# RMSNorm with Swish on one core: three engines from straight code to loops of three units, and the row sums shared out anew

## The chip, the core and the metric

The kernel runs on one core of a Trainium2 chip. The core has a matrix engine (TensorE), a vector engine (VectorE, DVE in the profile), an activation engine (ScalarE, ACT), a general engine (GpSimd, POOL) and SyncE (SP), which here only issues transfers. Each engine runs its own instruction stream; they meet through semaphores. Sixteen DMA engines move data between the chip's memory (HBM), where the inputs and the output lie, and the core's SBUF, 128 partitions wide. A small second memory, PSUM, also has 128 partitions.

The metric is the device time of one execution in microseconds, lower is better. One execution was also profiled; the profile's span runs from the first instruction to the last.

## The reference

```python
x = randn(16, 1024, 512)  # float32; gamma: ones(512); eps = 1e-5
rms = np.sqrt(np.mean(x ** 2, axis=-1, keepdims=True) + eps)
x_norm = x / rms * gamma
return x_norm * (1.0 / (1.0 + np.exp(-x_norm)))
```

There are 16,384 rows of 512 numbers, 2 KB each. Every row is divided by the root of its mean square, multiplied by gamma and passed through Swish, y·sigmoid(y), which the activation engine has as one function, Silu. 33.5 MB come in and 33.5 MB go out, and every row needs one sum and two passes over its data.

## The kernel before

Each partition works on 128 rows of its own, numbered 0 to 127 in the order in which they are worked on. The rows lie in HBM in four groups (`groups = [32, 48, 20, 28]`): in a group of n rows each partition has n neighbouring rows, so that a transfer of some of them is one contiguous piece per partition. SBUF holds a ring of 100 rows per partition (`xb`); row r lies at place r modulo 100. Everything is done in place: x is loaded into the ring, normalized there, passed through Silu there, and stored from there.

Four rows of every partition make a unit; there are 32 (`K`). A unit k goes through five steps:

- `square(k)` on ScalarE waits for the loads that the unit needs (L200). Two rows are squared one by one into PSUM with an accumulator that leaves their mean squares in `ms` (L203; the accumulator is read by an instruction of its own). The other two are squared together into a PSUM tile `sq` (L210).
- `sums(k)` on VectorE reduces that PSUM tile to the other two mean squares (L241).
- GpSimd adds eps (L184) and raises to the power -0.5 (L191), which gives `rstd` for four rows.
- `norm(k)` on VectorE multiplies each of the four rows by its rstd and by gamma (scalar_tensor_tensor, L252).
- `swish(k)` on ScalarE runs Silu over the four rows at once (L222).

All loops are Python loops, so that each engine has one long straight program. ScalarE's order is square(0), square(1), square(2), swish(0), square(3), swish(1) and so on; VectorE's is sums(0), sums(1), norm(0), sums(2), norm(1) and so on. Most waits are part of the waiting instruction and count upwards: `s_norm` at least k + 1, for instance. `ms`, `aeps` and `rstd` have a place for each unit; the PSUM tiles are two of each kind.

Three alignment directives stand at the head of the program (L151): the code of ScalarE, VectorE and GpSimd is placed at slots 8, 40 and 0 of a block of 128 instructions, and the engines jump there.

SyncE issues all data transfers in the written `order`. The first two loads go out ahead of the start-up barrier. Then come the loads up to row 79; SyncE waits until the load of row 48 has landed; store 0 (rows 0 to 31) goes out once 8 units are through Silu; then load 80. It waits until store 0 has been written, since the loads of rows 100 on reuse its places, and issues them. It waits until load 100 has landed, and then issues the other stores in order, each as soon as its units are through Silu (`ends`, L124): 16, 20, 25, 30 and 32 units for the stores of rows 32, 64, 80, 100 and 120. At the end it waits for all of them (L275). Gamma is read by a small transfer that ScalarE issues, and copied to all partitions by VectorE (L265).

Of the kernel before, what the change touches and what calls it, by code (L numbers as in the profile page):

```python
# [9 lines left out]
def kernel(  # L10
# [7 lines left out]
    nc = tc.nc  # L18
    P = nc.NUM_PARTITIONS
    AF = mybir.ActivationFunctionType  # L20
    ALU = mybir.AluOpType
    fp32 = mybir.dt.float32
# [2 lines left out]
    of = out.flatten_outer_dims()  # L25
    R, D = xf.shape

    groups = [32, 48, 20, 28]
    ring = 100
    loads = [(0, 4), (4, 4), (8, 8), (16, 8), (24, 8), (32, 16), (48, 27), (75, 5)]  # L30
    loads += [(80, 20), (100, 22), (122, 6)]
    stores = [(0, 32), (32, 32), (64, 16), (80, 20), (100, 20), (120, 8)]
    order = [("load", a) for a in (0, 4, 8, 16, 24, 32, 48, 75)]
    order += [("landed", 48), ("store", 0), ("load", 80)]
    order += [("stored", 0), ("load", 100), ("load", 122)]
    order += [("landed", 100)] + [("store", a) for a in (32, 64, 80, 100, 120)]
    early = 2
    cn = 4
    n_sq = 2

    first = [sum(groups[:g]) for g in range(len(groups))]
    rows_each = sum(groups)
# [6 lines left out]
        assert sum(n for _, n in pieces) == rows_each  # L49

    K = rows_each // cn
    load_at = {a: t for t, (a, _) in enumerate(loads)}
    store_at = {a: t for t, (a, _) in enumerate(stores)}
    landings, seen = [], 0
    for k in range(K):
        landings.append([])
        while seen < len(loads) and loads[seen][0] < (k + 1) * cn:
            landings[k].append(seen)
            seen += 1

    ends = [-(-(a + n) // cn) for a, n in stores]

    inv_d = 1.0 / float(D)
    eps_f = float(eps)
# [4 lines left out]
    def sbuf(name, shape, dt=fp32):  # L69
        return nc.alloc_sbuf_tensor(name, shape, dt).ap()  # L70

    xb = sbuf("xb", [P, ring, D])
    gamma4 = sbuf("gamma4", [P, D])
    gamma_sb = sbuf("gamma_sb", [P, D])
    neg_half = sbuf("neg_half", [P, cn])
    ms = sbuf("ms", [P, K, cn])
    aeps = sbuf("aeps", [P, K, cn])
    rstd = sbuf("rstd", [P, K, cn])
    sq = [nc.alloc_psum_tensor(f"sq{i}", [P, n_sq, D], fp32).ap() for i in range(2)]
    junk = [nc.alloc_psum_tensor(f"junk{i}", [P, D], fp32).ap() for i in range(2)]  # L80

    ld = [nc.alloc_semaphore(f"ld{t}") for t in range(len(loads))]
    st = [nc.alloc_semaphore(f"st{t}") for t in range(len(stores))]
# [5 lines left out]
    s_zero = nc.alloc_semaphore("s_zero")  # L89
    s_half = nc.alloc_semaphore("s_half")  # L90
    s_gamma = nc.alloc_semaphore("s_gamma")
    s_acc = nc.alloc_semaphore("s_acc")
    s_sq = nc.alloc_semaphore("s_sq")
    s_sum = nc.alloc_semaphore("s_sum")
    s_eps = nc.alloc_semaphore("s_eps")
    s_rstd = nc.alloc_semaphore("s_rstd")
# [2 lines left out]

    def need(ins, sem, value):  # L100
        return ins.wait_op(sem, value, "sem-ge")

    def dram(ap, piece):
        a, n = piece
# [6 lines left out]
    def buf(piece):  # L111
        a, n = piece
        at = a % ring
        assert at + n <= ring, piece
        return xb[:, at : at + n, :]
# [27 lines left out]

    entry = nc.main_func.blocks[0].instructions
    here = nc.cur_bb.bb.instructions
    for queue, engine, offset in (
        (nc.scalar, mybir.EngineType.Activation, 8),
        (nc.vector, mybir.EngineType.DVE, 40),
        (nc.gpsimd, mybir.EngineType.Pool, 0),
    ):  # L150
        ins = queue.addr_align(128, offset=offset, max_nops=0).ins  # L151
        assert here[-1] is ins or here[-1].name == ins.name
        here.pop()
        entry.insert(
            next(i for i, other in enumerate(entry) if other.engine == engine), ins
        )
    for t in range(early):
        ins = load(t).ins
        assert here[-1] is ins or here[-1].name == ins.name
# [7 lines left out]
    for what, a in order[early:]:  # L167
# [6 lines left out]
        else:  # L174
            nc.sync.wait_ge(st[store_at[a]], 16)
    nc.sync.wait_ge(s_scratch, 16)

    nc.gpsimd.memset(blank, 0.0).then_inc(s_blank, 1)  # L178
    nc.gpsimd.memset(gamma4, 0.0).then_inc(s_zero, 1)  # L179
    nc.gpsimd.memset(neg_half, -0.5).then_inc(s_half, 1)  # L180
    nc.gpsimd.wait_ge(s_half, 1)
    for k in range(K):
        need(
            nc.gpsimd.tensor_scalar(  # L184
                out=aeps[:, k, :], in0=ms[:, k, :], scalar1=eps_f, scalar2=None,
                op0=ALU.add,
            ),
            s_sum, k + 1,
        ).then_inc(s_eps, 1)
        need(  # L190
            nc.gpsimd.tensor_tensor(  # L191
                out=rstd[:, k, :], in0=aeps[:, k, :], in1=neg_half, op=ALU.pow
            ),
            s_eps, k + 1,
        ).then_inc(s_rstd, 1)

    def square(k):
        at = k * cn % ring
        for landing in landings[k]:
            nc.scalar.wait_ge(ld[landing], 16)  # L200
        for j in range(n_sq, cn):
            n = k * (cn - n_sq) + j - n_sq
            acc = nc.scalar.activation(  # L203
                out=junk[n % 2], in_=xb[:, at + j, :], func=AF.Square,
                scale=inv_d**0.5, accum_out=ms[:, k, j : j + 1],
            )
            if n >= 2:
                need(acc, s_acc, n - 1)
            acc.then_inc(s_acc, 1)
        square = nc.scalar.activation(  # L210
            out=sq[k % 2], in_=xb[:, at : at + n_sq, :],
            func=AF.Square, scale=inv_d**0.5,
        )
        if k >= 2:
            need(square, s_sum, k - 1)
        square.then_inc(s_sq, 1)

    def swish(k):
        at = k * cn % ring
        rows = xb[:, at : at + cn, :]  # L220
        need(
            nc.scalar.activation(out=rows, in_=rows, func=AF.Silu), s_norm, k + 1  # L222
        ).then_inc(s_swish, 1)

    need(nc.scalar.dma_start(out=scratch, in_=blank), s_blank, 1).then_inc(
        s_scratch, 16
# [3 lines left out]
        s_zero, 1,  # L230
    ).then_inc(s_gld, 16)
    nc.scalar.preload_act_table_set("silu_and_others")  # L232
    for k in range(K + 2):
        if k < K:
            square(k)
        if k >= 2:
            swish(k - 2)

    def sums(k):
        need(  # L240
            nc.vector.tensor_reduce(  # L241
                out=ms[:, k, 0:n_sq], in_=sq[k % 2], op=ALU.add,
                axis=mybir.AxisListType.X,
            ),
            s_sq, k + 1,
        ).then_inc(s_sum, 1)

    def norm(k):
        at = k * cn % ring
        for j in range(cn):  # L250
            row = xb[:, at + j, :]
            ins = nc.vector.scalar_tensor_tensor(  # L252
                out=row, in0=row, scalar=rstd[:, k, j : j + 1], in1=gamma_sb,
                op0=ALU.mult, op1=ALU.mult,
            )
            if j == 0:
                need(ins, s_rstd, k + 1)
        ins.then_inc(s_norm, 1)

    for k in range(K + 1):  # L260
        if k < K:
            sums(k)
        if k == 0:
            need(
                nc.vector.stream_shuffle(gamma_sb, gamma4, [0] * 32), s_gld, 16  # L265
            ).then_inc(s_gamma, 1)
        if k == 1:
            nc.vector.wait_ge(s_gamma, 1)
        if k >= 1:
            norm(k - 1)  # L270

    waited = {a for what, a in order if what == "stored"}
    for t, (a, _) in enumerate(stores):
        if a not in waited:
            nc.sync.wait_ge(st[t], 16)  # L275


# [33 lines left out]
```

## Time and profile before

| | |
|---|---|
| Median of 3 runs (lowest, highest) | 160.69 us (160.38, 160.9) |
| The profiled execution's own time | 160.84 us |
| Its span | 159.9 us |
| ScalarE busy | 129.4 us (81%) |
| VectorE busy | 124.4 us (78%) |
| GpSimd busy | 65.4 us (41%) |
| Moved by DMA | 67.17 MB, 420 GB/s over the span |
| Silu, 4 rows (L222) | 32 of 1904 ns |
| Square of one row with accumulator (L203) | 64 of 581 ns, and 64 accumulator reads of 186 ns |
| Square of two rows to PSUM (L210) | 32 of 1005 ns |
| Reduction of two rows (L241) | 32 of 1224 ns |
| scalar_tensor_tensor, one row (L252) | 128 of 746 ns |
| Add eps, power (L184, L191) | 32 of 644 ns, 32 of 1376 ns |
| SyncE's waits | 68.5 us for loads, 40.9 us for Silu, 22.4 us for store 0, 19.4 us at the end |

An instruction's duration runs from its start to its end; neighbours on one engine overlap a little, so that the distance from start to start is what one more instruction costs. The DMA share is the busy time of the DMA engines over sixteen times the length of a stretch; in short stretches it can pass 1, because a packet that is under way counts from its start to its end, and a DMA engine can have more than one. A transfer of 128 partitions is split over all sixteen DMA engines, eight partitions each, and lands when the last of the sixteen parts does.

### The profile page before, as it was taken

What the parts mean: (1) busy time and instruction counts of PE and PEld (TensorE: products, weight loads), DVE (VectorE), ACT (ScalarE), POOL (GpSimd) and SP (SyncE); (2) the same over time, 40 slices, a digit from 0 to 9 for tenths busy, and PEclk for the clock granted to TensorE, in tenths of its full rate; (3) what the DMA queues carried; (4) which work ended last, traced back from release to release, by engine and by line L of the source; (5) the groups of instructions that cost most, each with busy time, mean ns of one, the idle gap of its engine ahead of it and who ended that gap; (6) DMA issues with size and microseconds to landing.
All of it is one profiled execution on the core that took longest, in us unless ns stands there. A gap on an engine that the chain in (4) does not pass through costs nothing.

```text
span 159.9 us, 502 instructions
## 1 busy us (share of the span) xinstructions
DVE 124.4 (78%) x162; ACT 129.4 (81%) x193; POOL 65.4 (41%) x71
## 2 busy tenths in 40 slices
DVE  0059999999999999999999999999999999500000
ACT  0766999999999999999999999999999994800000
POOL 1035555555555555555555555555555555000000
DMA  7999999999979979988999899899699999899893
GB/s 252 440 424 434 430 496 393 494 443 443 429 326 513 492 328 492 479 346 348 481 444 439 372 430 555 370 443 508 295 484 410 393 486 461 379 471 440 389 410 135
DMA packets 2605, 67.17 MB, mean 420 GB/s; under 512 B 420, under 2 KB 420, under 8 KB 424
## 3 DMA queue, kind: packets, MB, share of 16 engines
q1 hardware_dynamic: 2448, 67.11, 97.9%
q10 hardware_dynamic: 152, 0.02, 0.1%
q14 instruction: 5, 0.04, 0.1%
HBM read 33.56 MB, written 33.56 MB: 420 GB/s over the span
## 4 chain that ended last, share of the span: by engine, by line
ACT 72%; DVE 6%; DMA 5%; issue 3%; POOL 0%; POOLq 0%
ACT xb L222 33%; ACT junk L203 22%; ACT sq L210 16%; DMA gamma<-in_gamma_dram 5%; DVE xb L252 5%; DVE ms L241 1%; DVE gamma_sb L265 0%; POOL gamma L179 0%; POOL blank L178 0%; POOLq L67 0%
## 5 line engine op out<-in xcount | busy, mean ns | idle before, releaser
L252 DVE SCALAR_TENSOR_TENSOR xb<-xb,rstd,gamma_sb 128x512 f32<-128x512 f32 x128 | 87.3, 746 | 0.0
L222 ACT ACTIVATE xb<-xb 128x2048 f32<-128x2048 f32 x32 | 60.9, 1904 | 3.2 <-DVE xb L252 3.2
L241 DVE TENSOR_REDUCE ms<-sq 128x2 f32<-128x1024 f32 x32 | 39.2, 1224 | 12.3 <-ACT sq L210 9.0
L184 POOL TENSOR_SCALAR aeps<-ms 128x4 f32<-128x4 f32 x32 | 20.6, 644 | 65.2 <-DVE ms L241 65.2
L191 POOL TENSOR_TENSOR rstd<-aeps,neg_half 128x4 f32<-128x4 f32 x32 | 44.0, 1376 | 2.7
L203 ACT ACTIVATE junk<-xb 128x512 f32<-128x512 f32 x64 | 37.2, 581 | 2.3 <-DMA xb<-in_x_dram 2.3
L210 ACT ACTIVATE sq<-xb 128x1024 f32<-128x1024 f32 x32 | 32.1, 1005 | 0.0
L203 ACT ACTIVATION_READ_ACCUMULATOR junk<-xb 128x1 f32 x64 | 11.9, 186 | 0.0
L232 ACT ACT_TABLE_LOAD x1 | 1.3, 1283 | 5.1 <-issue 5.1
L265 DVE LOAD_MASK_SELECT gamma_sb<-gamma x1 | 0.0, 14 | 1.3 <-DMA gamma<-in_gamma_dram 1.3
L265 DVE STREAM_SHUFFLE gamma_sb<-gamma 128x512 f32<-128x512 f32 x1 | 0.7, 716 | 0.0
L178 POOL MEMSET blank<- 128x16 f32 x1 | 0.1, 111 | 1.1 <-POOLq L67 1.1
L179 POOL MEMSET gamma<- 128x512 f32 x1 | 0.5, 524 | 0.0
L292 POOL MEMSET const-float32-0.0<- 128x1 f32 x1 | 0.1, 98 | 0.7 <-issue 0.7
L292 POOL MEMSET const-bfloat16-1.0<- 128x1 bf16 x1 | 0.1, 102 | 0.0
L292 POOL MEMSET const-uint8-127<- 128x1 uint8 x1 | 0.1, 102 | 0.0
L180 POOL MEMSET neg_half<- 128x4 f32 x1 | 0.1, 101 | 0.0
L292 POOL MEMSET const-float32-1.0<- 128x1 f32 x1 | 0.1, 98 | 0.0
## 6 DMA issues: line engine op xcount, KB each, us to landing
out_dram<-xb SPq DMA_DIRECT2D x2, 5120.0 KB, 25.6
xb<-in_x_dram SPq DMA_DIRECT2D x1, 6912.0 KB, 44.9
xb<-in_x_dram SPq DMA_DIRECT2D x3, 2048.0 KB, 15.6
xb<-in_x_dram SPq DMA_DIRECT2D x1, 5632.0 KB, 25.4
xb<-in_x_dram SPq DMA_DIRECT2D x1, 5120.0 KB, 34.9
xb<-in_x_dram SPq DMA_DIRECT2D x1, 4096.0 KB, 29.1
out_dram<-xb SPq DMA_DIRECT2D x1, 4096.0 KB, 32.9
xb<-in_x_dram SPq DMA_DIRECT2D x2, 1024.0 KB, 6.6
```

The lines of the kernel that those rows point to most:

```text
L178: nc.gpsimd.memset(blank, 0.0).then_inc(s_blank, 1)
L179: nc.gpsimd.memset(gamma4, 0.0).then_inc(s_zero, 1)
L184: nc.gpsimd.tensor_scalar(out=aeps[:, k, :], in0=ms[:, k, :], scalar1=eps_f, scalar2=None, op0=ALU.add,),
L191: nc.gpsimd.tensor_tensor(out=rstd[:, k, :], in0=aeps[:, k, :], in1=neg_half, op=ALU.pow),
L203: acc = nc.scalar.activation(out=junk[n % 2], in_=xb[:, at + j, :], func=AF.Square, scale=inv_d**0.5, accum_out=ms[:, k, j : j + 1],)
L210: square = nc.scalar.activation(out=sq[k % 2], in_=xb[:, at : at + n_sq, :], func=AF.Square, scale=inv_d**0.5,)
L222: nc.scalar.activation(out=rows, in_=rows, func=AF.Silu), s_norm, k + 1
L232: nc.scalar.preload_act_table_set("silu_and_others")
L241: nc.vector.tensor_reduce(out=ms[:, k, 0:n_sq], in_=sq[k % 2], op=ALU.add, axis=mybir.AxisListType.X,),
L252: ins = nc.vector.scalar_tensor_tensor(out=row, in0=row, scalar=rstd[:, k, j : j + 1], in1=gamma_sb, op0=ALU.mult, op1=ALU.mult,)
L265: nc.vector.stream_shuffle(gamma_sb, gamma4, [0] * 32), s_gld, 16
L292: nc = _bacc.Bacc("TRN2", target_bir_lowering=False, num_devices=1)
```

## The change

ScalarE, VectorE and GpSimd get loops that run ten times, with three units in the body (U = 3); the first and last units stand outside. Ring places are computed in registers on ScalarE and VectorE. A count that grows with k can't be a constant in a loop, so each wait becomes an instruction of its own that waits for at least 1 and takes 1 off (`take`). TensorE, idle before, waits for each load and adds the number of units that have become complete to `s_land`, which ScalarE takes one at a time.

The sums are shared out anew: ScalarE squares and sums three rows of a unit, one by one, with accumulators; VectorE sums the fourth with a scalar_tensor_tensor of the row with itself and an accumulator. The squares of two rows to PSUM and the reduction from it are gone. The small tiles `ms`, `aeps` and `rstd` are three of each, used in turn; what the sums write besides (`junk`, `junk_v`) has twelve places, four of them in SBUF.

The ring has 96 rows, the last two groups 16 and 32 rows, and the later transfers are cut to fit: loads of 16, 26 and 6 rows from rows 80, 96 and 122, stores of 16, 24 and 8 rows from rows 80, 96 and 120. The store of row 96 needs 30 units. The alignment directives are gone.

```diff
--- before.py
+++ after.py
@@ -25,18 +25,17 @@
     of = out.flatten_outer_dims()
     R, D = xf.shape
 
-    groups = [32, 48, 20, 28]
-    ring = 100
+    groups = [32, 48, 16, 32]
+    ring = 96
     loads = [(0, 4), (4, 4), (8, 8), (16, 8), (24, 8), (32, 16), (48, 27), (75, 5)]
-    loads += [(80, 20), (100, 22), (122, 6)]
-    stores = [(0, 32), (32, 32), (64, 16), (80, 20), (100, 20), (120, 8)]
+    loads += [(80, 16), (96, 26), (122, 6)]
+    stores = [(0, 32), (32, 32), (64, 16), (80, 16), (96, 24), (120, 8)]
     order = [("load", a) for a in (0, 4, 8, 16, 24, 32, 48, 75)]
     order += [("landed", 48), ("store", 0), ("load", 80)]
-    order += [("stored", 0), ("load", 100), ("load", 122)]
-    order += [("landed", 100)] + [("store", a) for a in (32, 64, 80, 100, 120)]
+    order += [("stored", 0), ("load", 96), ("load", 122)]
+    order += [("landed", 96)] + [("store", a) for a in (32, 64, 80, 96, 120)]
     early = 2
     cn = 4
-    n_sq = 2
 
     first = [sum(groups[:g]) for g in range(len(groups))]
     rows_each = sum(groups)
@@ -49,15 +48,11 @@
         assert sum(n for _, n in pieces) == rows_each
 
     K = rows_each // cn
+    U = 3
+    rounds = (K - 2) // U
+    assert U * rounds == K - 2
     load_at = {a: t for t, (a, _) in enumerate(loads)}
     store_at = {a: t for t, (a, _) in enumerate(stores)}
-    landings, seen = [], 0
-    for k in range(K):
-        landings.append([])
-        while seen < len(loads) and loads[seen][0] < (k + 1) * cn:
-            landings[k].append(seen)
-            seen += 1
-
     ends = [-(-(a + n) // cn) for a, n in stores]
 
     inv_d = 1.0 / float(D)
...
-    ms = sbuf("ms", [P, K, cn])
-    aeps = sbuf("aeps", [P, K, cn])
-    rstd = sbuf("rstd", [P, K, cn])
-    sq = [nc.alloc_psum_tensor(f"sq{i}", [P, n_sq, D], fp32).ap() for i in range(2)]
-    junk = [nc.alloc_psum_tensor(f"junk{i}", [P, D], fp32).ap() for i in range(2)]
+    ms = [sbuf(f"ms{u}", [P, cn]) for u in range(U)]
+    aeps = [sbuf(f"aeps{u}", [P, cn]) for u in range(U)]
+    rstd = [sbuf(f"rstd{u}", [P, cn]) for u in range(U)]
+    junk = [nc.alloc_psum_tensor(f"junk{i}", [P, D], fp32).ap() for i in range(8)]
+    junk.append(sbuf("junk8", [P, D]))
+    junk_v = [sbuf(f"junk_v{u}", [P, D]) for u in range(U)]
 
...
+    s_land = nc.alloc_semaphore("s_land")
...
-    s_sq = nc.alloc_semaphore("s_sq")
...
+    def take(queue, sem):
+        queue.wait_ge(sem, 1).then_inc(sem, -1)
...
-    for queue, engine, offset in (
-        (nc.scalar, mybir.EngineType.Activation, 8),
-        (nc.vector, mybir.EngineType.DVE, 40),
-        (nc.gpsimd, mybir.EngineType.Pool, 0),
-    ):
-        ins = queue.addr_align(128, offset=offset, max_nops=0).ins
-        assert here[-1] is ins or here[-1].name == ins.name
-        here.pop()
-        entry.insert(
-            next(i for i, other in enumerate(entry) if other.engine == engine), ins
-        )
...
+    waited = {a for what, a in order if what == "stored"}
+    for t, (a, _) in enumerate(stores):
+        if a not in waited:
+            nc.sync.wait_ge(st[t], 16)
+
+    passed = 0
+    for t, (a, n) in enumerate(loads):
+        units = (a + n) // cn
+        nc.tensor.wait_ge(ld[t], 16).then_inc(s_land, units - passed)
+        passed = units
+    assert passed == K
...
-    for k in range(K):
-        need(
-            nc.gpsimd.tensor_scalar(
-                out=aeps[:, k, :], in0=ms[:, k, :], scalar1=eps_f, scalar2=None,
-                op0=ALU.add,
-            ),
-            s_sum, k + 1,
+
+    def rsqrt(u):
+        take(nc.gpsimd, s_sum)
+        nc.gpsimd.tensor_scalar(
+            out=aeps[u], in0=ms[u], scalar1=eps_f, scalar2=None, op0=ALU.add,
         ).then_inc(s_eps, 1)
-        need(
-            nc.gpsimd.tensor_tensor(
-                out=rstd[:, k, :], in0=aeps[:, k, :], in1=neg_half, op=ALU.pow
-            ),
-            s_eps, k + 1,
+        take(nc.gpsimd, s_eps)
+        nc.gpsimd.tensor_tensor(
+            out=rstd[u], in0=aeps[u], in1=neg_half, op=ALU.pow
         ).then_inc(s_rstd, 1)
 
-    def square(k):
-        at = k * cn % ring
-        for landing in landings[k]:
-            nc.scalar.wait_ge(ld[landing], 16)
-        for j in range(n_sq, cn):
-            n = k * (cn - n_sq) + j - n_sq
+    rsqrt(0)
+    rsqrt(1)
+    with nc.gpsimd.Fori(0, rounds, 1):
+        for j in range(U):
+            rsqrt((2 + j) % U)
+
+    def rows_of(queue, v, j, n=1):
+        return xb[:, bass.ds(queue.snap(v + j, min_val=0, max_val=ring - n), n), :]
+
+    def row_of(queue, v, j):
+        if isinstance(v, int):
+            return xb[:, v + j, :]
+        return rows_of(queue, v, j).rearrange("p n d -> p (n d)")
+
+    def square(u, rows):
+        take(nc.scalar, s_land)
+        for j in range(cn - 1):
             acc = nc.scalar.activation(
-                out=junk[n % 2], in_=xb[:, at + j, :], func=AF.Square,
-                scale=inv_d**0.5, accum_out=ms[:, k, j : j + 1],
+                out=junk[u * (cn - 1) + j], in_=rows[j], func=AF.Square,
+                scale=inv_d**0.5, accum_out=ms[u][:, j : j + 1],
             )
-            if n >= 2:
-                need(acc, s_acc, n - 1)
-            acc.then_inc(s_acc, 1)
-        square = nc.scalar.activation(
-            out=sq[k % 2], in_=xb[:, at : at + n_sq, :],
-            func=AF.Square, scale=inv_d**0.5,
-        )
-        if k >= 2:
-            need(square, s_sum, k - 1)
-        square.then_inc(s_sq, 1)
-
-    def swish(k):
-        at = k * cn % ring
-        rows = xb[:, at : at + cn, :]
-        need(
-            nc.scalar.activation(out=rows, in_=rows, func=AF.Silu), s_norm, k + 1
-        ).then_inc(s_swish, 1)
+        acc.then_inc(s_acc, 1)
+
+    def swish(rows):
+        take(nc.scalar, s_norm)
+        nc.scalar.activation(out=rows, in_=rows, func=AF.Silu).then_inc(s_swish, 1)
 
...
-    for k in range(K + 2):
-        if k < K:
-            square(k)
-        if k >= 2:
-            swish(k - 2)
-
-    def sums(k):
-        need(
-            nc.vector.tensor_reduce(
-                out=ms[:, k, 0:n_sq], in_=sq[k % 2], op=ALU.add,
-                axis=mybir.AxisListType.X,
-            ),
-            s_sq, k + 1,
+    at = [nc.scalar.alloc_register(f"at{j}") for j in range(U)]
+    nc.scalar.reg_mov(at[1], 0)
+    nc.scalar.reg_mov(at[2], cn)
+    for k in range(2):
+        square(k, [xb[:, k * cn + j, :] for j in range(cn)])
+    with nc.scalar.Fori(0, rounds, 1):
+        for j in range(U):
+            now, old = at[j], at[(j + 1) % U]
+            nc.scalar.reg_alu(now, at[(j + 2) % U], cn, op=ALU.add)
+            nc.scalar.reg_alu(now, now, ring, op=ALU.mod)
+            v = nc.scalar.snap(now, min_val=0, max_val=ring - cn)
+            square((2 + j) % U, [row_of(nc.scalar, v, i) for i in range(cn)])
+            w = nc.scalar.snap(old, min_val=0, max_val=ring - cn)
+            swish(xb[:, bass.ds(w, cn), :])
+    for k in range(K - 2, K):
+        swish(buf((k * cn, cn)))
+
+    def sums(u, row):
+        take(nc.vector, s_acc)
+        nc.vector.scalar_tensor_tensor(
+            out=junk_v[u], in0=row, scalar=inv_d, in1=row,
+            op0=ALU.mult, op1=ALU.mult, accum_out=ms[u][:, cn - 1 : cn],
         ).then_inc(s_sum, 1)
 
-    def norm(k):
-        at = k * cn % ring
+    def norm(u, rows):
+        take(nc.vector, s_rstd)
         for j in range(cn):
-            row = xb[:, at + j, :]
             ins = nc.vector.scalar_tensor_tensor(
-                out=row, in0=row, scalar=rstd[:, k, j : j + 1], in1=gamma_sb,
-                op0=ALU.mult, op1=ALU.mult,
+                out=rows[j], in0=rows[j], scalar=rstd[u][:, j : j + 1],
+                in1=gamma_sb, op0=ALU.mult, op1=ALU.mult,
             )
-            if j == 0:
-                need(ins, s_rstd, k + 1)
         ins.then_inc(s_norm, 1)
 
-    for k in range(K + 1):
-        if k < K:
-            sums(k)
-        if k == 0:
-            need(
-                nc.vector.stream_shuffle(gamma_sb, gamma4, [0] * 32), s_gld, 16
-            ).then_inc(s_gamma, 1)
-        if k == 1:
-            nc.vector.wait_ge(s_gamma, 1)
-        if k >= 1:
-            norm(k - 1)
-
-    waited = {a for what, a in order if what == "stored"}
-    for t, (a, _) in enumerate(stores):
-        if a not in waited:
-            nc.sync.wait_ge(st[t], 16)
+    to = [nc.vector.alloc_register(f"to{j}") for j in range(U)]
+    nc.vector.reg_mov(to[2], cn)
+    sums(0, xb[:, cn - 1, :])
+    need(nc.vector.stream_shuffle(gamma_sb, gamma4, [0] * 32), s_gld, 16).then_inc(
+        s_gamma, 1
+    )
+    sums(1, xb[:, 2 * cn - 1, :])
+    nc.vector.wait_ge(s_gamma, 1)
+    norm(0, [xb[:, j, :] for j in range(cn)])
+    with nc.vector.Fori(0, rounds, 1):
+        for j in range(U):
+            now, old = to[j], to[(j + 2) % U]
+            nc.vector.reg_alu(now, old, cn, op=ALU.add)
+            nc.vector.reg_alu(now, now, ring, op=ALU.mod)
+            v = nc.vector.snap(now, min_val=0, max_val=ring - cn)
+            sums((2 + j) % U, row_of(nc.vector, v, cn - 1))
+            w = nc.vector.snap(old, min_val=0, max_val=ring - cn)
+            norm((1 + j) % U, [row_of(nc.vector, w, i) for i in range(cn)])
+    norm((K - 1) % U, [buf(((K - 1) * cn + j, 1))[:, 0, :] for j in range(cn)])
 
 
 # ---- launch: one core; inputs and outputs as the reference has them ----
```

## The prediction

> **What bounds the kernel now.** I read the page first, for which resource is full, then the DMA shares by stretch of time, then SyncE's waits and issues, then one unit of work on each engine. The page's slices of the span, with DMA on the second row of digits and GB/s left out here, and its queue rows:
>
> ```profile
> ACT  0766999999999999999999999999999994800000
> ...
> DMA  7999999999979979988999899899699999899893
> ...
> q1 hardware_dynamic: 2448, 67.11, 97.9%
> ...
> q14 instruction: 5, 0.04, 0.1%
> ```
>
> The DMA engines are full from the first slice to the last and their data queue took 97.9% of sixteen engines' span, while ScalarE stops five slices before the end. So compute costs time only where a late store or load leaves the DMA engines empty. The windows 1:40, 40:80, 80:120 and 120:157 moved 436, 423, 434 and 426 GB/s: no stage has a hole. The end looks different (columns: window, its length, three engines' busy time, clock, DMA share of 16 engines, GB/s):
>
> ```profile
> 156.50:157.00 0.50, 0.00 (x0) 0.00 (x0) 0.00 (x0) 1.00 1.07 459
> 157.00:157.50 0.50, 0.00 (x0) 0.00 (x0) 0.00 (x0) 1.00 0.32 131
> 157.50:158.00 0.50, 0.00 (x0) 0.00 (x0) 0.00 (x0) 1.00 0.15 66
> 158.00:158.50 0.50, 0.00 (x0) 0.00 (x0) 0.00 (x0) 1.00 0.08 33
> 158.50:159.00 0.50, 0.00 (x0) 0.00 (x0) 0.00 (x0) 1.00 0.08 33
> ```
>
> A share of 0.08 is 1.3 engines of 16: most DMA engines are done at 157.5, and one or two work on alone for about two microseconds. The landing events say the same: the sixteen parts of the last store land at 157.43 to 158.20 (fourteen), 158.69 and 159.90, with a median of 157.64. That straggler, 2.3 us behind the median, ends the span.
>
> SyncE's issues, in the order of the timeline (start, length, what):
>
> ```profile
> 48.94 0.35 SPq L124 DMA_DIRECT2D out_dram<-xb  x1
> ...
> 133.39 0.33 SPq L124 DMA_DIRECT2D out_dram<-xb  x1
> ...
> 140.05 0.33 SPq L124 DMA_DIRECT2D out_dram<-xb  x1
> ```
>
> These are store 0, the second-to-last store (20 rows) and the last (8 rows). One unit on ScalarE in steady state:
>
> ```profile
> 99.53 1.90 ACT L222 ACTIVATE xb<-xb 128x2048 f32<-128x2048 f32 x1
> 101.33 0.58 ACT L203 ACTIVATE junk<-xb 128x512 f32<-128x512 f32 x1
> 101.86 0.19 ACT L203 ACTIVATION_READ_ACCUMULATOR junk<-xb 128x1 f32 x1
> 101.95 0.58 ACT L203 ACTIVATE junk<-xb 128x512 f32<-128x512 f32 x1
> 102.47 0.19 ACT L203 ACTIVATION_READ_ACCUMULATOR junk<-xb 128x1 f32 x1
> 102.56 1.01 ACT L210 ACTIVATE sq<-xb 128x1024 f32<-128x1024 f32 x1
> 103.52 1.91 ACT L222 ACTIVATE xb<-xb 128x2048 f32<-128x2048 f32 x1
> ```
>
> From start to start: Silu 1.80, two summed rows 0.62 and 0.61, the two-row square 0.96, in all 3.99 us a unit, without a gap. Thirty-two of them run under 156 us of transfers.
>
> **When compute matters.** A row of all partitions takes 0.604 us of DMA time (from the landings of the 16-row to those of the 20-row store, 128.43 to 140.50). Most DMA engines end at 157.5. After the change the last two stores have 24 and 8 rows, 19.3 us, so the first of them has to start by 138.2. From issue to first packet went 1.45 us (97.60 to 99.05 for the store of row 32), so it has to be issued by 136.7. It waits for 30 units; before, unit 29's Silu ended at 133.39 and unit 0's at 17.61. The margin is 3.3 us (it was 5.7 with 20 rows), and the pace at which it is used up is (136.7 - 17.6)/29 = 4.11 us a unit. The last store, due by 151.2, came at 140.05. Store 0 was ready at 45.5 and waited for a load until 48.94; it allows a later unit 7, too.
>
> **The change, part by part.**
>
> ScalarE: the two-row square (0.96) goes and a third summed row (0.61) comes: 1.80 + 3 x 0.61 = 3.64 a unit. VectorE: the reduction (1.14 from start to start, 47.71 to 48.85) becomes one more scalar_tensor_tensor with an accumulator, by the four others 0.66 to 0.75: about 2.83 + 0.7 = 3.5 in place of 3.97. Its accumulator read is not in the trace; the nearest row, ScalarE's, is 0.19, with 0 as the low end, so at most 3.7. GpSimd keeps its two operations, 0.66 + 1.39 = 2.05. Hand-offs: a wait was part of the instruction (norm's end to Silu's start 0.03); now it is an instruction of its own. ScalarE's separate wait on a load shows the price: landed 13.01, wait 13.03, ACTIVATE 13.09, so 0.08. Two hand-offs lie in the ring sums(k-1), norm(k-2), Silu(k-2), squares(k) that spans two units: 0.16 + 0.75 + 2.73 + 1.80 + 1.84 = 7.3, or 3.64 a unit. I take 3.8, for what registers add; below 4.11 it is worth nothing either way, because DMA covers it.
>
> Register and address instructions: I count some 15 a unit on ScalarE and 18 on VectorE, none of them in the old trace. Low end: 0.017, as an event instruction runs. Usual end: 0.08, the distance of two of them on GpSimd (1.39 to 1.47): 18 x 0.08 = 1.4, behind 2.73 of norms. Far end: 0.33, as SyncE's issue: 6 us a unit, which nothing hides. I take 0.08, the instruction most like them, and nothing for the loop's branch, which as a compare-and-branch ran 0.03 to 0.05 here.
>
> Other moves, at nothing, with their cover: load 80 shrinks from 20 to 16 rows, which cover the wait for store 0 (over at 72.11, next packets 73.6); it would land at about 81.8 in place of 84.2, so 8 us of cover stays. Units 24 on now come with load 96, which ends on the same row as load 100 did and so lands at 97.5; their squares began at 101.33, or at a pace of 3.8 near 96.7, a wait under 1 us that the margin of 3.3 takes. TensorE passes landings on: one hand-off of 0.08. The start stays: ScalarE's table load ends at 6.35, gamma lands at 11.17, rows 8 on at 13.0. The three alignment branches ran 0.03 to 0.05 beside SyncE's first issue at 0.00.
>
> Instruction fetches: this is where I look for the gain. The trace's packet records put the five packets of 8 KB at 2.74, 2.78, 3.25, 65.95 and 67.96, each 0.31 us on a DMA engine that has no spare time. ScalarE had about 106 records and VectorE 80 before 66, which with their alignment offsets of 8 and 40 makes about 120: both then enter a second block of 128 instructions, and the next is fetched. The last part's lag behind the median follows: 1.0 us at load 75 (51.93 against 50.9), 1.5 at store 0 (72.11 against 70.65), 1.5 at load 100, then, with no fetch near, 2.2 at load 122 (101.88 against 99.65), 2.3 at the end. So the two later fetches brought about 0.45, the three early ones at most 1.0, and 0.75 is unexplained. Loops need far less code, and without the jump onto aligned blocks the early fetches are not forced. I take one fetch less on the straggler: 0.45, and 0.15 of the early 1.0. The ends are 0 and 1.45.
>
> Sum against the profiled execution: 159.9 span + 0.94 around it = 160.84, less 0.6 = 160.24. That execution is 0.15 above the median of 160.69, so 160.1.
>
> **A rule that speaks against it.** The row is those five packets of 8 KB. The Trainium skill, "Runtime: NRT & Kernel Launch", section "Instruction fetch mechanics", says that prefetch is sequential and that a taken branch to a target outside the current two-page window stalls for a fetch. It gives pages of 16 KiB; the packets here are 8 KB, so the trace disagrees on size and, all executing forward, cannot test the stall. With its page a body of some 75 instructions rarely crosses a boundary and the sum stays 160.1; with the trace's block it often does, and the sum is the first rival's.
>
> **Rivals.**
> (1) Slower: the loop refetches its code. A body of about 75 instructions on ScalarE, 68 on VectorE, placed anywhere in blocks of 128, lies across a boundary with a chance near 0.6. If going on into the second block has the third fetched over the first, every back edge misses. Price: from the branch at 0.12 to the next block's packet done at 3.06 is 2.9 us; the Silu in hand (1.9) covers part, so 1.0 to 2.9 each, ten times, 0.33 to 0.97 a unit on 3.8: pace 4.1 to 4.8. At 4.3 the store is issued at 142.3, 5.6 late: 166. Ten to twenty more packets at 0.31 to 0.43 also load one DMA engine by 3 to 9 us: 163 to 169. Both blocks missed each round: beyond 175. It decides from the first back edge on. For it: nothing pins the bodies. Against: no fetch stalled an engine in the old trace.
> (2) Slower by pace alone: registers cost more than 0.23 each (4.11/18), nothing overlapping. At 4.3 again 166; at 4.11 nothing. Against: every sequencer row but the DMA issues is below 0.08.
> (3) The tail isn't the fetches': 0.75 of it came with none near. Then it stays, 160.7, within 160.2 to 161.2.
>
> **How the numbers follow.** Forecast 0.52, its own range 159.1 to 160.7; (1) 0.26; (2) 0.11; (3) 0.11. A difference of 0.3%, 0.48 us, is about the least that can be told here. Of the forecast 0.35 is under 160.2, 0.15 within and 0.02 above; of (3) 0.02, 0.06, 0.03; of (2) 0.02 within and 0.09 above; all of (1) above. Faster 0.37, same 0.23, slower 0.40. Range: 159.1 leaves out 0.05 of the forecast; 169 leaves out some 0.13 of the first two rivals.
>
> **What would show it.** Right: instruction packets below five, none repeated; ScalarE's Silus 3.6 to 4.0 apart until loads hold them; the store of row 96 issued before 136.7; the last windows' lone share shorter than 2 us. Wrong: dozens of instruction packets and "issue" gaps of 1 to 3 us every third unit (1); steady gaps between ScalarE's instructions (2); five packets or fewer and the same tail (3).

## The result, and the profile after

The changed kernel takes 160.31 us (median of 20 runs, 159.91 to 161.22), the kernel before 160.90 in runs beside it (20, 160.38 to 161.27). The ratio is 0.9972, with a 95% interval of 0.996 to 0.9984: faster by 0.28%. That ratio is one of means; the medians differ by 0.59 us, 0.36%, so the change is about as large as the 0.3% that the prediction called the least that can be told. The prediction was 160.1, faster, with a range of 159.1 to 169; it gave "faster" a chance of 0.37, less than "slower".

The profiled execution took 159.91 us with a span of 158.6. The page's slices and queue rows, for ScalarE and DMA:

```profile
ACT  0836999999999999999999999999999954000000
...
DMA  7999999999969969979999999996989999999976
...
q1 hardware_dynamic: 2448, 67.11, 98.7%
...
q14 instruction: 2, 0.02, 0.0%
```

ScalarE stops more than a slice earlier than before, the DMA engines are as full as they were, and the data queue's share rises from 97.9 to 98.7% only because the span is shorter. Two instruction packets are left of five. The end, in the same windows as before the change (window, length, busy times, clock, DMA share, GB/s):

```profile
157.00:157.50 0.50, 0.00 (x0) 0.00 (x0) 0.00 (x0) 1.00 0.17 66
157.50:158.00 0.50, 0.00 (x0) 0.00 (x0) 0.00 (x0) 1.00 0.00 0
```

The lone share of 0.08 from 158 to 159 is gone. By the landing events of the last store, the median of its sixteen parts lands at 157.67, where it landed before (157.66), and the last part 0.88 us after it in place of 2.25. Most of the sixteen parts land as they did; the three ahead of the last are 0.2 to 0.4 us nearer to the median, and the last is 1.37 us nearer.

A unit on ScalarE, in the timeline:

```profile
98.80 1.89 ACT L217 ACTIVATE xb<-xb  x1
100.60 0.58 ACT L209 ACTIVATE junk<-xb 128x512 f32 x1
101.12 0.19 ACT L209 ACTIVATION_READ_ACCUMULATOR junk<-xb 128x1 f32 x1
101.22 0.58 ACT L209 ACTIVATE junk<-xb 128x512 f32 x1
101.74 0.19 ACT L209 ACTIVATION_READ_ACCUMULATOR junk<-xb 128x1 f32 x1
101.83 0.58 ACT L209 ACTIVATE junk<-xb 128x512 f32 x1
102.35 0.19 ACT L209 ACTIVATION_READ_ACCUMULATOR junk<-xb 128x1 f32 x1
102.70 1.91 ACT L217 ACTIVATE xb<-xb  x1 [0.17 <-ACTq L100]
```

Silu 1.80 and three squares of 0.61 to 0.62, then a gap of 0.17 that ends with the separate wait (L100 is `take`). From the first Silu's end (17.21) to the thirtieth's (127.29) the pace is 3.80 us a unit, before 3.99. The store of row 96 was issued at 127.31:

```profile
127.31 0.33 SPq L123 DMA_DIRECT2D out_dram<-xb  x1
```

One thing had not been looked for. Time minus span is 0.89 in the profiled execution of before and 1.31 in this one. (The prediction's 0.94 came from a span rounded to 159.9; the trace has 159.95.) The median over the runs is 0.89 for the kernel before, in its runs on other chips, and 1.32 for the changed kernel. So the span fell by about 1.0 us, from some 160.0 (160.90 less 0.89, since the spans of these runs of before are not on record) to a median of 159.0; 0.43 came back outside it, and the time fell by 0.59.

### The profile page after: what moved, and what is told of

It is laid out like the page before. It is cut to its first block, busy times and chain, and to the rows that moved or that the text cites. A ratio compares the mean times of both kernels' runs of the same rounds, so it can differ in the third digit from the quotient of the medians.

```text
span 158.6 us, 1330 instructions
## 1 busy us (share of the span) xinstructions
DVE 107.9 (68%) x194; ACT 121.1 (76%) x225; POOL 59.3 (37%) x71
## 3 DMA queue, kind: packets, MB, share of 16 engines
q1 hardware_dynamic: 2448, 67.11, 98.7%
## 5 line engine op out<-in xcount | busy, mean ns | idle before, releaser
L254 DVE SCALAR_TENSOR_TENSOR xb<-xb,rstd,gamma_sb 128x512 f32 (+1 forms) x128 | 87.5, 747 | 0.1
L217 ACT ACTIVATE xb<-xb (+1 forms) x32 | 61.1, 1908 | 4.8 <-ACTq L100 4.2
L209 ACT ACTIVATE junk<-xb 128x512 f32 (+1 forms) x96 | 56.1, 585 | 4.0 <-ACTq L100 3.9
L188 POOL TENSOR_TENSOR rstd<-aeps,neg_half 128x4 f32<-128x4 f32 x32 | 40.9, 1279 | 5.9 <-POOLq L100 5.9
L184 POOL TENSOR_SCALAR aeps<-ms 128x4 f32<-128x4 f32 x32 | 17.6, 550 | 61.5 <-POOLq L100 61.5
L246 DVE SCALAR_TENSOR_TENSOR junk_v<-xb 128x512 f32 (+1 forms) x32 | 22.1, 692 | 20.1 <-DVEq L100 20.1
L209 ACT ACTIVATION_READ_ACCUMULATOR junk<-xb 128x1 f32 x96 | 17.9, 186 | 0.0
L246 DVE DVE_READ_ACCUMULATOR junk_v<-xb 128x1 f32 x32 | 2.7, 83 | 0.0
```

Source lines behind the costliest of these rows:

```text
L184: nc.gpsimd.tensor_scalar(out=aeps[u], in0=ms[u], scalar1=eps_f, scalar2=None, op0=ALU.add,).then_inc(s_eps, 1)
L188: nc.gpsimd.tensor_tensor(out=rstd[u], in0=aeps[u], in1=neg_half, op=ALU.pow).then_inc(s_rstd, 1)
L209: acc = nc.scalar.activation(out=junk[u * (cn - 1) + j], in_=rows[j], func=AF.Square, scale=inv_d**0.5, accum_out=ms[u][:, j : j + 1],)
L217: nc.scalar.activation(out=rows, in_=rows, func=AF.Silu).then_inc(s_swish, 1)
L246: nc.vector.scalar_tensor_tensor(out=junk_v[u], in0=row, scalar=inv_d, in1=row, op0=ALU.mult, op1=ALU.mult, accum_out=ms[u][:, cn - 1 : cn ...
L254: ins = nc.vector.scalar_tensor_tensor(out=rows[j], in0=rows[j], scalar=rstd[u][:, j : j + 1], in1=gamma_sb, op0=ALU.mult, op1=ALU.mult,)
```

## The experiments

Theory 1 was the prediction's: each instruction packet costs one DMA engine time, and the changed kernel has fewer. Its rivals: the ring and the pieces of the transfers (theory 2), or the new sums, shorten the tail; or the directives alone do. In the tables below, "lag" is how far the last part of the last store lands behind the median part in the profiled execution, "out" is the median of time minus span over the runs, and spans are medians over the runs. Several chips were used, and the kernel before differs between them, so each run stands against the kernel before on its own chip.

**The directives, the ring and the loops, one at a time.** The first kernel takes the directives out of the kernel before, and nothing else:

```diff
-    for queue, engine, offset in (
-        (nc.scalar, mybir.EngineType.Activation, 8),
-        (nc.vector, mybir.EngineType.DVE, 40),
-        (nc.gpsimd, mybir.EngineType.Pool, 0),
-    ):
...
```

> The kernel before without its three alignment directives, nothing else changed. Theory 1 (instruction packets delay single DMA engines): the three packets at 2.7 to 3.3 us are gone; straight code still crosses blocks, 3 or 4 packets later on; the last part of the last store lands 0.9 to 1.5 us behind the median in place of 2.25, span 158.5 to 159.2. Theory 2 (the shorter tail comes from the ring and the pieces of the transfers): five packets or fewer, lag still 2.2, span 159.9. In both, if the directives also decide when the measured time starts, the time exceeds the span by 1.3 in place of 0.94 us: 159.8 to 160.5 by theory 1, 161.2 by theory 2; if they do not, by 0.94.

The second gives the kernel before the new ring and pieces:

```diff
-    groups = [32, 48, 20, 28]
-    ring = 100
+    groups = [32, 48, 16, 32]
+    ring = 96
...
```

> The kernel before with the ring, the groups, the loads and stores of the changed kernel alone; straight code and directives stay. Theory 1 (instruction packets): same five packets, lag of the last part 2.2 us, time as before, 160.9. Theory 2 (ring and pieces): lag 0.9 us, span 158.6, time 159.5.

The third puts the directives back into the changed kernel:

```diff
+    for queue, engine, offset in (
+        (nc.scalar, mybir.EngineType.Activation, 8),
+        (nc.vector, mybir.EngineType.DVE, 40),
+        (nc.gpsimd, mybir.EngineType.Pool, 0),
+    ):
...
```

> The changed kernel with the old alignment directives put back. Theory 1: three packets at 2.7 to 3.3 us, none later, since the looped code ends inside its blocks (by a count of instructions, ScalarE at slot 97, VectorE at 124); lag of the last part near 0.95 from the first load to the last store, so the span stays within 0.1 of the changed kernel's. If the jump delays the start of the measured time, time minus span falls from 1.31 to 0.94 and the time is 159.9 to 160.0; if not, 160.3 to 160.4.

The fourth writes the changed kernel's loops out:

```diff
-    with nc.scalar.Fori(0, rounds, 1):
...
+    for k in range(2, K):
+        square(k % U, [xb[:, k * cn % ring + i, :] for i in range(cn)])
+        swish(buf(((k - 2) * cn, cn)))
```

> The changed kernel with its three loops written out: same sums, ring, waits, no directives. Theory 1: ScalarE and VectorE cross two block boundaries each, GpSimd one, five packets; lag of the last part 1.5 to 2.2 us, time 160.9 to 161.6. If the loops are not what shortens the tail but the sums or the ring: lag 0.9 and 160.3.

All four ran on one chip, with the kernel before at 160.95 (span 160.1):

| Kernel | time | ratio to before | span | out | 8 KB packets at | lag |
|---|---|---|---|---|---|---|
| before, no directives | 160.17 | 0.9955 [0.9939, 0.9972] | 158.85 | 1.29 | 39, 43, 73, 112 | 0.90 |
| before, new ring | 160.92 | 0.9997 [0.9985, 1.001] | 160.05 | 0.88 | 2.8, 3.0, 3.4, 66, 68 | 2.51 |
| changed, with directives | 160.68 | 0.9985 [0.9967, 1.0003] | 159.55 | 1.14 | 2.8, 2.8, 3.2 | 1.59 |
| changed, written out | 161.27 | 1.0018 [0.9999, 1.0036] | 159.95 | 1.32 | 30, 37, 58, 86, 99 | 2.59 |

The queue rows of the pages, first of before without directives, then of the changed kernel with them:

```profile
q14 instruction: 4, 0.03, 0.1%
```

```profile
q14 instruction: 3, 0.02, 0.0%
```

Theory 2 falls: the new ring alone changes nothing. In straight code the directives are the whole gain: against the kernel before on its chip, the straight kernel without them is as fast as the changed one (0.9955 against 0.9972), with four packets against two. So the number of packets isn't what matters, as theory 1 had it in this form. In the changed kernel the case is less clear. With the directives put back its median span is still 0.5 below that of the straight kernel with the same ring and the same directives (resampling the runs gives 0.05 to 0.9), though its time can't be told from that kernel's. It did not run beside the changed kernel on one chip, and its 160.68 lies above all that was expected of it. Written out, the changed kernel loses its gain (1.0018 against 0.9972); that its five packets are the reason, one of them at 99.4, is argued, since the step described below falls at the same place.

What a packet costs can be read from the packet records of all these traces. The data packet that starts just as an instruction packet ends takes 0.16 to 0.65 us longer than others of its size: after the packet at 65.95 a packet of 64 KB takes 2.89 in place of 2.42, after the changed kernel's at 27.33 one of 32 KB takes 1.82 in place of 1.21. With the instruction packet's own 0.31 that is 0.5 to 1.0 us for one DMA engine, more than the prediction's 0.31.

Which packets set the end is harder. In the kernel before, the three between 2.7 and 3.3 us put three parts 0.55, 0.66 and 0.94 behind the median by the first load's landing, and the last is still 0.97 behind at load 75. But the changed kernel with directives has the same three, with 0.94 at load 75, and by load 96 its last part is 0.70 behind, just as in the changed kernel without them (0.70) and in the straight kernel without them (0.70). In the kernel before it is 1.38 behind at store 0 and 1.56 at load 100, and what that trace has besides are the packets at 66 and 68. So in these traces the early packets alone do not last to the end; the later two make the difference, and it is the directives in straight code that put them there. How the lag of the early ones shrinks between load 75 and load 96 was not found: none of these four traces has fewer than 15 packets under way at any time between 5 and 157 us, so it is not that the others run out of work. At the end four parts of the straight kernel without directives are 0.75 to 0.90 behind, while the kernel before has one at 2.25 and the next at 1.03. That looks like losses on four engines there and several on one engine here; the traces do not name the engine of a packet, so this is not shown.

That the out column falls from 1.3 to 0.88 with directives in straight code fits with where the engines begin: the trace has the first instructions of ScalarE, VectorE and GpSimd at 0.13 without them and, after the jump, at 0.56 to 0.66 with them, while SyncE's first load is issued at 0.00 in both, and the last event comes 1.42 to 1.43 after the span's end in every trace. So without the jump some 0.43 us more of the start seems to be counted, though the loads run no later. The changed kernel with directives has 1.14, between the two.

**Where the measured time starts, and shorter code.** One addition to the kernel before:

```diff
+    for t in range(len(loads)):
+        nc.tensor.wait_ge(ld[t], 16)
```

> The kernel before, directives in place, with one addition: TensorE waits for each load and does nothing else. Theory A (the measured time starts with the first instruction of any engine that the program uses except SyncE; TensorE, which has no directive, begins at 0.31, the others after their jump at 0.56): time minus span rises from 0.89 to 1.14, span unchanged at 160.1, time 161.2. Theory B (TensorE plays no part in when time starts): time minus span 0.89, time 160.95.

It took 160.59 against 160.61 (ratio 1.0 [0.999, 1.001]), span 159.7, out 0.88. The time minus the span stayed as it was, so TensorE plays no part; the 1.14 of the changed kernel with directives stays unexplained.

The changed kernel with addresses from the loop's counter:

```diff
-            now, old = at[j], at[(j + 1) % U]
-            nc.scalar.reg_alu(now, at[(j + 2) % U], cn, op=ALU.add)
-            nc.scalar.reg_alu(now, now, ring, op=ALU.mod)
...
+        v = (i * (U * cn) + (c * cn + j)) % ring
+        return xb[:, bass.ds(v, n), :]
```

> The changed kernel with the ring places computed from the loop's counter in one instruction per operand, no registers kept from unit to unit: 14 instructions less on ScalarE and on VectorE (71 and 66 in place of 85 and 80 from the program's start). Theory 1 (each instruction packet costs one DMA engine time): the two packets of 22.4 and 27.3 us came where the code crossed a block boundary, by their times near the 76th instruction, so the shorter code has none; lag of the last part 0.2 to 0.3 us throughout, span 158.0 to 158.4, time minus span 1.31, time 159.3 to 159.7. If the lag of 0.88 has another cause: 160.2 to 160.4.

It was a miss: 160.70 against 160.61 (1.0005 [0.9992, 1.0018]), span 159.4 against 159.7, lag 1.59. On this chip the kernel before is 0.3 to 0.4 us faster than in the other sets of runs, and its near relative with TensorE's waits has a lag of 1.63, not 2.25. Neither relative of the changed kernel that could have kept the gain, this one and the one with one square in three below, was faster than the kernel before there. The changed kernel itself did not run on this chip, so whether it gains anything there is open. One packet of 8 KB came at 27.2 and one at 134.2, after ScalarE's work was nearly done. But most of the lag did not come from them. It was 0.17 at store 0 (landed at 70.5) and 1.34 at load 80 (80.1), with no packet in between. What stands there is SyncE: it issued two loads back to back at 70.74 and 71.11. That these are the cause is not shown.

**The second source of lag.** The lag of the last part at load 96 (100 in the kernel before), and then at load 122, four microseconds later, in the traces: before 1.56, 2.21; before with new ring 1.52, 2.49; changed with directives 0.70, 1.55; changed kernel 0.70, 0.70 in the first profile and 0.79, 1.65 in a later one; before without directives 0.70, 0.81 and 0.67, 1.33. No instruction packet is near. What the records do show are 12 KB packets of load 122 that take 0.25 us or more beyond their usual 0.46 (0.77 more in the kernel before); where the step is absent, in the changed kernel's first profile, there is none. Just there, at 97, SyncE issues the stores of rows 32 and 64 back to back. One kernel separates them:

```diff
-    order += [("landed", 96)] + [("store", a) for a in (32, 64, 80, 96, 120)]
+    order += [("landed", 96), ("store", 32), ("landed", 122)]
+    order += [("store", a) for a in (64, 80, 96, 120)]
```

> The changed kernel with the store of row 64 issued only once load 122 has landed, so that SyncE no longer issues two stores back to back at 97 us; nothing else changed. In several traces one DMA engine lost 0.6 to 0.95 us just after that pair, with no instruction packet near. If the pair of issues is the cause: no such step at load 122, span 0.2 to 0.5 below the changed kernel's. If not: span the same within 0.2, and the step can still be there.

Beside it on the same chip ran both candidates again:

> The changed kernel as it is, beside the next two on one chip, because the kernel before has been 160.95 on the chip of the first four runs and 160.61 on that of the next four. If the gain is the removal of the directives and of their early packets: span 0.7 to 1.1 below the kernel before's, time 0.3 to 0.7 below. If the gain hangs on the chip: time within 0.2 of the kernel before's, as two near relations of it were on the second chip (160.69 and 160.70 against 160.61).

> The kernel before without its directives, again. If dropping the directives is the whole gain: within 0.2 us of the changed kernel on the same chip. If the loops and the sums bring something of their own: at least 0.3 above it.

The kernel before was 160.99 there (span 160.1):

| Kernel | time | ratio to before | span | out | lag at 96, 122, end |
|---|---|---|---|---|---|
| changed | 160.65 | 0.9977 [0.9963, 0.9991] | 159.35 | 1.30 | 0.79, 1.65, 1.73 |
| before, no directives | 160.44 | 0.9962 [0.9948, 0.9977] | 159.1 | 1.33 | 0.67, 1.33, 1.41 |
| changed, stores apart | 160.19 | 0.9955 [0.9938, 0.9971] | 158.9 | 1.30 | 0.78, 0.79, 1.02 |

SyncE's issues in the changed kernel and in the one with the stores apart (start, length from the first to the last issue, what):

```profile
96.82 0.82 SPq L123 DMA_DIRECT2D out_dram<-xb  x2
```

```profile
96.99 4.02 SPq L124 DMA_DIRECT2D out_dram<-xb  x2
```

and their ends, in the same order:

```profile
157.50:158.00 0.50, 0.00 (x0) 0.00 (x0) 0.00 (x0) 1.00 0.15 66
158.00:158.50 0.50, 0.00 (x0) 0.00 (x0) 0.00 (x0) 1.00 0.08 33
```

```profile
157.50:158.00 0.50, 0.00 (x0) 0.00 (x0) 0.00 (x0) 1.00 0.16 66
158.00:158.50 0.50, 0.00 (x0) 0.00 (x0) 0.00 (x0) 1.00 0.00 0
```

With the stores apart the step is gone and the median span is 0.45 lower than the changed kernel's (resampling the runs gives 0.1 to 0.7). That is the expected 0.2 to 0.5, and the lowest median on this chip. The step did not appear in every trace that has the pair, so one trace without it proves little by itself; the spans carry the verdict that the new order helps. They do not show that the pair is the cause. In the trace of the next kernel, with a square more in every unit, SyncE issued the two stores 1.53 us apart, and the step was there all the same (1.13 at load 96, 2.03 at load 122). What the new order also does is to keep the store of row 64 out until load 122 has landed; which of the two counts, and why, was not found. The straight kernel without directives is not above the changed one on this chip either (0.2 below, within the scatter): in straight code their removal is enough for the gain, here as on the first chip.

**Whether compute has the slack that the prediction gave it.** One square more on ScalarE, its result unused, in every unit or in one of three (`cond` is `True` or `u == 0`):

```diff
         take(nc.scalar, s_land)
+        if cond:
+            nc.scalar.activation(
+                out=more[u], in_=rows[0], func=AF.Square,
+                scale=inv_d**0.5, accum_out=msx[u],
+            )
```

> The changed kernel with one more square of a row on ScalarE in every unit, its result unused: 0.61 us a unit. By the due time of the prediction (the store of row 96 issued by 136.7, 30 units needed, issued at 127.3 so far): it is issued near 145, DMA engines stand idle for some 8 us, time 167 to 169.5. If compute does not decide when the stores go: 160.3.

> The same additional square in one unit of three, 0.2 us a unit on average. The store of row 96 is issued at 132 to 134, still ahead of 136.7: time as the changed kernel's, 160.2 to 160.5. If pace costs time even below the due: about 4 us more, 164.

One in three: 160.69 against 160.61 for the kernel before (1.0001 [0.999, 1.0013]), the store of row 96 at 131.89, ahead of 136.7, the median part of the last store at 157.47. The time was expected at 160.2 to 160.5; the changed kernel did not run on that chip, but its relative there, the one with shorter code and without the squares, took 160.70. In every unit: 163.08 (1.0151 [1.0132, 1.0171]), not 167 to 169.5. The store was issued at 141.21, because 0.45 us a unit more, not 0.61, reached the pace (4.25 against 3.80):

```profile
141.21 0.33 SPq L125 DMA_DIRECT2D out_dram<-xb  x1
```

Here the DMA engines do stand idle:

```profile
136.00:138.00 2.00, 2.00 (x6) 2.00 (x5) 1.54 (x2) 1.00 0.80 344
138.00:140.00 2.00, 1.10 (x3) 2.00 (x7) 0.31 (x1) 1.00 0.08 33
140.00:142.00 2.00, 2.00 (x5) 1.18 (x1) 1.29 (x2) 1.00 0.00 0
142.00:144.00 2.00, 2.00 (x4) 0.89 (x1) 0.56 (x1) 1.00 1.72 737
```

The issue came 141.2 - 136.7 = 4.5 us late, and the median part of the last store landed at 161.92 in place of 157.47 with one square in three on the same chip, 4.45 later: the due time holds to 0.1 us. The span rose less, since the pause let the straggler catch up: its lag fell from 1.99 at the store of row 80 to 0.08 at the store of row 96.

**Whether loops refetch their code.** Two directives inside ScalarE's loop, ahead of the second and third unit of the body:

```diff
+            if j:
+                nc.scalar.addr_align(128, offset=0, max_nops=0)
             now, old = at[j], at[(j + 1) % U]
```

> The changed kernel with two alignment directives inside ScalarE's loop, so that its body of about 53 instructions lies in at least three blocks of 128 in place of two. If the engine holds no more than three blocks and fetches the next one over the oldest: every round fetches blocks again, 20 to 40 packets, gaps of 1 to 3 us on ScalarE each round, time 165 or more. If it holds four or more: at most 6 packets, time 160.3 to 160.9.

161.07 against 160.99 (1.0005 [0.9989, 1.002]), 0.4 above the changed kernel on the same chip and above the expected 160.3 to 160.9, but nowhere near 165. The page counts:

```profile
q14 instruction: 3, 0.02, 0.0%
```

They came at 19.5, 24.4 and 28.5, and never again in ten rounds. The Silus kept their pace (the thirtieth ended at 127.99). No refetch, even over three blocks or more. What the one packet more and the jumps cost in the 0.4 us was not taken apart.

## Why the prediction was right, and where it was not

**The bound.** Right. The DMA engines stay full; the last store's median part lands at 157.66 before and 157.67 after. The faster pace of compute (3.80, as taken) is worth nothing, and a unit every 3.95 (the square in one unit of three) costs nothing that can be seen.

**Register and address instructions.** Right as a bound, with the price now visible: on ScalarE an address operation ran 0.055, an arithmetic one 0.038, a move 0.029 (VectorE 0.069, 0.045, 0.036), within the 0.08 taken, and there were fewer of them than counted, 8 a unit in place of 15 (VectorE 9 in place of 18). The hand-off was dearer than the 0.08 taken: from the norms' end to Silu 0.20 in the loop and 0.12 behind it, from the add to the power on GpSimd 0.18.

**The due time, 136.7 and 4.11 us a unit.** Right as a mechanism, shown by the extra squares: no cost to be seen at 131.9, a last store 4.45 us later for 4.5 us of lateness. The time rose by only some 2.4 us over its relatives on that chip, since the straggler caught up.

**Instruction fetches, "one fetch less on the straggler: 0.45, and 0.15 of the early 1.0".** The direction was right, the size was not, and part of the rest was luck. The tail shrank by more, 1.37 us in the lag of the first profile and 0.75 to 1.0 in median span. By load 96 (100 in the kernel before) the lag is down from 1.56 to 0.70: 0.86 for the 0.60 taken. The term's 0.45 for a fetch is at the low end of what one packet costs in these records, 0.5 to 1.0, since the data packet behind it loses time too. Another 0.65 of the 1.37 is the step at load 122, the place of most of the "0.75 unexplained". The changed kernel has that step too, in its second profile; the first was one without it. That makes the profiled gain of 0.93 larger than that of the medians, 0.59. "Loops need far less code" is one way to the gain and not the only one, since straight code without the directives gains as much. That the early fetches go with the jump was the second half of the same sentence and also came true, but no run shows what their going is worth by itself: with them put back the lag at load 96 is 0.70 all the same. The packets that the kernel before has beyond these are the two at 66 and 68.

**The alignment directives at nothing.** Wrong: the sum kept what lies around the span, and it rose from 0.89 to 1.32. This is a term of 0.4 us that the prediction did not have. It offset the 0.4 that the span fell beyond the sum's 0.6, and so 160.1 came close to 160.31 by two errors of opposite sign, which is luck.

**Rival 1, refetching.** Its chance near 0.6 that a body lies across a boundary was fair: packets came at 22 and 27 us, while the first round ran, and not later. The chance of 0.26 was spent on the other half, that the third block replaces the first, and that is refuted by the body over three blocks. The Trainium skill's "Runtime: NRT & Kernel Launch", section "Instruction fetch mechanics", has a window of two pages of 16 KiB. By that figure, four of the 8 KB blocks seen here would be as much memory, an estimate; every run with loops agrees with that, with two or three packets each, and none here is long enough to show where it ends.

**Rival 2** had its price below 4.11 right (nothing); its cause did not come, since no register operation ran near 0.23. Its 166 at a pace of 4.3 was too much: at 4.25 the extra squares took 163.08. **Rival 3**, that part of the tail isn't the fetches', was half true: the step at load 122 is 0.65 of it.

## What to carry to other kernels

Where all DMA engines are full, as here, the last of sixteen parts sets the end: read the landings part by part before the averages, since a lag of 1 to 2 us of one part does not show in a share of 98%. A directive that places code can cost data time far from any engine it concerns, by when it makes instruction packets arrive, and what it costs is found by taking it out alone. One trace is one draw of such losses: compare the medians of the runs before explaining a tail. Give an engine's work a due time from the transfers behind it; below that pace its instructions are free, and above it only the lateness counts.

## What the runs showed of the hardware

- A loop body across a boundary of 128 instructions, or over at least three such blocks, was fetched once in ten rounds (two and three packets of 8 KB, the last at 28.5 us).
- An 8 KB instruction packet takes 0.31 to 0.32 us of one DMA engine in most cases (0.45 and 0.55 in two), and the data packet that starts as it ends takes 0.16 to 0.65 us longer than others of its size.
- After SyncE issued the stores of rows 32 and 64 within 0.4 us at 97, most traces show a further lag of 0.56 us or more on one part by load 122, and 12 KB packets that took 0.25 us or more beyond 0.46. With 1.5 us between the two stores the step was there too (0.90); with 3.7 us, the second behind load 122's landing, it was not, in the one kernel that did so. The cause is open.
- Where the three compute engines began 0.43 us later, after a jump, the time measured for straight code was 0.4 us nearer to the span, while the transfers ran as before. With loops and the jump it was 0.18 nearer, which is open.
